# Sixteen more first products of the experts per layer, made during the routing and kept in DRAM until their dense step

## The chip, the cores and the metric

One Trainium2 chip, one core, one launch. The metric is the time of the program on the device in microseconds (us). The engines are TensorE (PE in the rows; PEld is its weight loads), VectorE (DVE), ScalarE (ACT), GpSimd (POOL) and SyncE (SP), which issues most of the DMAs.

## The reference, cut to what matters

Two layers: a token mixer, then PEER, a channel mixer that picks experts by product keys. For each block of 128 tokens and each of 8 heads:

```python
q = (xt @ w_q).reshape(n, PEER_HEADS, 2, PEER_DHALF)
s = jnp.einsum('nhpd,hpkd->nhpk', q, keys)
sv, si = lax.top_k(s, PEER_TOPK)                 # 16 of 128, twice
cand = sv[:, :, 0, :, None] + sv[:, :, 1, None, :]
cs, ci = lax.top_k(cand.reshape(n, PEER_HEADS, -1), PEER_TOPK)
gate = jax.nn.softmax(cs, axis=-1)               # 16 of 16384 experts a head
a = jnp.einsum('nd,nhkd->nhk', xt, u[eidx])      # first product
w = gate * jax.nn.gelu(a, approximate=False)
return jnp.einsum('nhk,nhkd->nd', w, v[eidx])    # second product
```

There are 512 latent and, in layer 0, 256 context tokens.

## The kernel before

**Two ways for the experts.** Three of the four latent blocks (384 tokens, ND) are computed *densely*, for all 16384 experts, in 128 steps of 128 experts. The fourth latent block, and in layer 0 the two context blocks, *gather* the rows of u and v that were chosen: gather(), one "row" at a time, which is an indirect DMA of 512 KB from GpSimd into a ring of five buffers (uv) and one VectorE operation on it (junkv, line 1023, for u; pacc, line 1036, for v). A block has 256 rows; layer 0 has 768 in all, layer 1 256.

**One dense step j.** The *first product* z = gelu(u_j x) has 24 matmuls of 384 columns in three passes (proj2, line 217): weights and tokens are each split into two parts, hi (a cast on ScalarE) and lo (a subtraction on GpSimd or VectorE). Then dense_w multiplies z by the gates (dz, line 1168) and splits the result into dw (1171, 1172). The *second product* adds w v_j into six PSUM banks, dacc, with 18 matmuls of 512 columns (dense_v, line 1178). The first product runs 21 steps (layer 0) or 28 steps (layer 1) ahead of the second, since the first 18 or 27 (UPRE) are made during the routing and wait in SBUF in dz tiles; they get their gelu in dense_w, in place. The last 4 steps' second products are done block by block at the end.

**The stages of peer().** (1) route(): query projections, top-k of the scores, the selection (select(), tiles named sel, dgt, fij) and, for each of the three dense blocks, gate_build(), which makes the dense gate matrix with 32 *units* of two matmuls gds and four gps, and writes it to DRAM (gd). That makes 96 units a layer; below they are counted from 1. Behind it in the program come the UPRE first products (tiles wraw, whi, wlo, dA). beside() lets 78 rows of layer 0 (GROWS) run next to the 96 units. (2) The dense steps; each releases further rows by a quota, behind its dw. (3) A residual add (hm, hr), the next layer's norms, keys and values.

**What sets the order.** All of it is written once in program order; the framework then orders each engine's instructions by a simulated timeline and by priority. So the order on an engine is fixed before the run, and an engine takes its instructions strictly one after the other: what stands behind a waiting instruction waits too. Sixty-four rows (LATE) of layer 0 are left for the next layer's mixer.

Of the kernel before, what the change touches and what calls it, by code (L numbers as in the profile page):

```python
# [9 lines left out]
F32 = mybir.dt.float32  # L10
# [12 lines left out]
ND = 384  # L23
# [5 lines left out]
GROWS = 78, 0  # L29
# [2 lines left out]
NLAT = 5  # L32
FIRST = 1, 1, 0, 1, 0, 1, 0, 1, 0, 1, 0, 1, 1, 0, 0, 0
XA, VPRE = 2, 2
UEXT = 3, 1
TAIL = 4
GEND = 124
# [73 lines left out]
class Kern:  # L111
    def __init__(self, ctx, tc, a, dbg=None):
        self.ctx, self.tc, self.nc, self.a = ctx, tc, tc.nc, a
        self.dbg = dbg or {}
        E = ctx.enter_context
        self.pc = E(tc.tile_pool(name="cst", bufs=1, reuse_waits="tile"))
        self.pg = E(tc.tile_pool(name="gat", bufs=1, reuse_waits="tile"))
        self.px = self.xt = E(tc.tile_pool(name="xt", bufs=1, reuse_waits="tile"))
        self.dr = E(tc.tile_pool(name="dr", bufs=1, space=bass.MemoryType.DRAM))
        self.wk = None  # L120
        nc = self.nc
        self.tables()
        self.cst = self.pc.tile([128, CST_N], F32, name="cst")
        self.ident = self.c("ident")
        self.eps = self.pc.tile([128, 1], F32, name="eps")
        nc.vector.memset(self.eps, EPS)
        self.one = self.c("ones")[:, 0:1]
        self.modd = self.dr.tile([2, 2, 6 * D], F32, name="modd")
        self.hd = self.dr.tile([768, D], F32, name="hd")
        self.x2d = self.dr.tile([768, D], F32, name="x2d")  # L130
        self.h1 = self.dr.tile([768, D], F32, name="h1")
        self.gd = self.dr.tile([ND // 16, 128, 128, 16], F32, name="gd")
        self.yd = self.dr.tile([2, D, 768], F32, name="yd")
        self.bd = self.dr.tile([ND // 128, 1024, 256], BF16, name="bd")

    def consts(self):
# [979 lines left out]
    def halves(self, src, shape, eng):  # L1116
# [6 lines left out]
        eng.tensor_tensor(lo, raw, hi.bitcast(F32), op=OP.subtract)  # L1123
        return hi, lo

    def dense_u(self, j, u, A, xt):


        nc = self.nc
        self.proj2(A, u, xt, ND)  # L1130
        if j % (self.ahead + 1) <= self.upre:
            z = self.dz.tile([128, ND], F32, name="dz", tag="dz", bufs=self.upre + 1)
        else:
            z = self.dn.tile([128, ND], F32, name="dz", tag="dze", bufs=self.ahead - self.upre)
        if j < self.ahead:
            nc.scalar.copy(z, A)
        else:
            nc.scalar.activation(z, A, AF.Gelu)  # L1138
        return z
# [3 lines left out]
        return self.halves(self.a["pr_v"][r:r + 128, :], [D], self.nc.vector)  # L1143

    def ahead_u(self, l, n, pda, xt, z, eng):
        u = self.halves(self.a["uT"][l, n], [8, 128], eng)
        A = pda.tile([128, ND], F32, name="dA", tag="dA", bufs=2)
        z[n] = self.dense_u(n, u, A, xt)
# [10 lines left out]
    def dense_w(self, j, z):  # L1159
        nc = self.nc  # L1160
        JG = self.jg
        if j > 0 and j % JG == 0:
            self.load_gates(j, range(3))
        if j < self.ahead:
            with self.tc.issue_after(self.lastexp.ins):
                nc.scalar.activation(z, z, AF.Gelu)
        z3 = z.rearrange("p (c t) -> p c t", t=16)
        nc.vector.tensor_tensor(z3, z3, self.G[:, :, j % JG, :], op=OP.mult)  # L1168
        wh, wl = (self.dn.tile([128, ND], F32R, name="dw", tag="dw" + x, bufs=2) if j < 128 - TAIL else
                  self.dz.tile([128, ND], F32R, name="dw", tag="dz", bufs=self.upre + 1) for x in "hl")  # L1170
        nc.scalar.copy(wh, z)  # L1171
        i = nc.vector.tensor_tensor(wl, z, wh.bitcast(F32), op=OP.subtract)  # L1172
        return wh, wl, i
# [166 lines left out]
    def peer(self, l, xt, bb, gat, rows, done, late, put):  # L1340

        tc, nc = self.tc, self.nc
        PS = bass.MemoryType.PSUM
        nd = ND // 128
        nb = 4
        upre = self.upre = UPRE[l]
        self.ahead = upre + UEXT[l]
        self.jg = JGS[l]  # L1350
        with tc.tile_pool(name="dz", bufs=1, reuse_waits="tile") as self.dz:
            with self.mixing(), self.phase("rt"):
                pool, tag = ((self.wk, "sel"), (self.pg, "uv"))[l]
                alloc = lambda: pool.tile([128, D], F32, name="sel", tag=tag, bufs=5)
                self.gate_consts()
                step = [0]

                def beside(hot):

                    step[0] += 1  # L1360
                    if step[0] * GROWS[l] // 96 > (step[0] - 1) * GROWS[l] // 96:
                        with tc.issue_after(hot.ins):
                            next(rows)

                sel = self.route(l, xt, nb, nd, alloc, lambda *a: self.gate_build(*a, beside))
                if l == 0:
                    self.mod(1, [0, 1])
                z = {}
                for j in range(upre):
                    u = self.parts(self.weight(self.a["uT"][l, j], [128, 8, 128]), (nc.gpsimd, nc.vector)[j % 2])  # L1370
                    z[j] = self.dense_u(j, u, self.pj([128, ND], "dA"), xt)
            gat += [(bb + b, LAT, sel[b]) for b in range(nd, nb)]
            left, done = 256 * len(gat) - done - GROWS[l] - late, 0
            with tc.tile_pool(name="dn", bufs=1, reuse_waits="tile") as self.dn, \
                    tc.tile_pool(name="pda", bufs=1, space=PS, reuse_waits="tile") as pda, \
                    self.phase("d2"), tc.tile_pool(name="pd", bufs=1, space=PS, reuse_waits="tile") as pd:
                acc = [pd.tile([128, 2, 512], F32, name="dacc%d" % b) for b in range(nd)]
                self.load_gates(0, [0, 1])
                for n in range(upre, self.ahead):
                    self.ahead_u(l, n, pda, xt, z, (nc.gpsimd, nc.vector)[(n - upre) % XA])  # L1380
                vs = {n: self.v_rows(l, n) for n in range(VPRE)}
                self.load_gates(0, [2])
                w = {0: self.dense_w(0, z.pop(0))}
                last = []
                for j in range(128):
                    if j + self.ahead < 128:
                        self.ahead_u(l, j + self.ahead, pda, xt, z, nc.gpsimd)
                    if j == TJ:
                        self.tables(True)
                    if j + 1 < 128:  # L1390
                        w[j + 1] = self.dense_w(j + 1, z.pop(j + 1))
                    wj = w.pop(j)
                    v = vs.pop(j) if j in vs else self.v_rows(l, j)
                    if j < 128 - TAIL:
                        for b in range(nd):
                            self.dense_v(j, b, wj, v, acc)
                    else:
                        last.append((j, wj, v))
                    with tc.issue_after(wj[2].ins):
                        while done < min(left * (j + 2) // GEND, left):  # L1400
                            next(rows)
                            done += 1
                for b in range(nd):
                    for j, wj, v in last:
                        self.dense_v(j, b, wj, v, acc)
                m5 = self.row5(l, LAT)
                for b in range(nd):
                    put(bb + b, self.resid(m5, acc[b].rearrange("p h d -> p (h d)"), bb + b))
# [139 lines left out]
```

## Time and profile before

| | |
|---|---|
| timed runs | 4202.59, 4206.1, 4202.59 us (median 4202.59) |
| profiled execution | 4207.51 us, span 4205.7 us |
| busy | PE 91%, PEld 78%, DVE 79%, POOL 54%, ACT 36% of the span |
| chain that ended last | PE 58%, DVE 16%, DMA 11%, issue 8%, POOL 6% |
| layer 0: gate units, dense steps | 1162 to 1387 us, 1420 to 2405 us |
| layer 1: gate units, dense steps | 3036 to 3237 us, 3245 to 4199 us |

The busy share is a mean over stages with different limits. A matmul's duration overlaps the next one's, so the price of matmuls is read from how many pass in a stretch without a gap.

### The profile page before, as it was taken

Reading aid. Unit: us, or ns where it says so; the run is one execution under the profiler, and the core shown is the slowest. Engines: PE = TensorE matmul, PEld = TensorE weight load, DVE = VectorE, ACT = ScalarE, POOL = GpSimd, SP = SyncE. Lnnn points to the kernel's source line nnn. Section 1 sums busy time; section 2 is a strip of 40 time slices with the busy share of each in tenths; the row PEclk is TensorE's granted clock in tenths of the full one; section 3 lists DMA queues with packets and bytes.
Section 4 is the critical chain, followed back from the end, with each engine's and each line's share of the span. In section 5 each row is a group of like instructions: output and inputs, shape, how many; then the busy total and the mean of one; then the engine's idle time right before and its main releaser. Section 6 shows DMA issues by size and latency. Waiting matters only on the chain.

```text
span 4205.7 us, 56328 instructions
## 1 busy us (share of the span) xinstructions
PE 3816.9 (91%) x19774; PEld 3259.6 (78%) x19780; DVE 3316.6 (79%) x5835; ACT 1508.1 (36%) x2746; POOL 2261.8 (54%) x1644
## 2 busy tenths in 40 slices
PE   8988776769888799999999889999989999999999
PEld 5776554547777699988999767777877899999987
DVE  4359888866998899989999987537875977777788
ACT  3322322312146333333333324332356333333333
POOL 1016777542454587877888563004531666666664
PEclk9999888879999999999999999999999999999999
DMA  5556898783449999999999995423346988787878
GB/s 192 172 200 209 308 322 307 253 287 121 149 161 398 367 332 334 332 324 333 346 339 331 341 333 194 158 85 111 111 160 235 346 279 285 275 290 273 282 268 313
DMA packets 389674, 1099.30 MB, mean 261 GB/s; under 512 B 32959, under 2 KB 140807, under 8 KB 383246
## 3 DMA queue, kind: packets, MB, share of 16 engines
q0 software_dynamic: 147456, 536.94, 35.2%
q1 hardware_dynamic: 232142, 497.95, 34.6%
q10 hardware_dynamic: 9792, 60.82, 3.5%
q8 instruction: 155, 2.54, 0.2%
q14 instruction: 129, 1.06, 0.1%
HBM read 1024.18 MB, written 71.40 MB: 260 GB/s over the span
## 4 chain that ended last, share of the span: by engine, by line
PE 58%; DVE 16%; DMA 11%; issue 8%; POOL 6%; ACT 2%; SPq 0%; ACTq 0%; POOLq 0%; DVEq 0%
PE dacc L1178 20%; PE dA L217 18%; POOL uv L1010 4%; DMA uv<-in_pr_u_dram,ix 3%; PE ops L223 3%; DMA uv<-in_pr_v_dram,ix 3%; PE pqps L217 2%; DVE junkv L1023 2%; PE gps L1108 2%; DMA draw<-in_uT_dram 1%; PE oo L1335 1%; DVE pacc L1036 1%; PE gds L1091 1%; PE modps L252 1%; PE oqps L210 1%
## 5 line engine op out<-in xcount | busy, mean ns | idle before, releaser
L1178 PE MATMUL dacc<-dhi,dw 128*128 128x512 f32 x3072 | 983.7, 390 | 3.4 <-ACT dw L1171 1.9
L1010 POOL DMA_INDIRECT uv<-in_pr_u_dram,ix x512 | 669.4, 1307 | 447.7 <-DVE pa L1023 316.0
L1010 POOL DMA_INDIRECT uv<-in_pr_v_dram,ix x512 | 680.0, 1328 | 408.0 <-DVE pacc L1036 281.9
L1023 DVE CUSTOM_DVE_ANT_0 junkv<-uv,x 128x1024 bf16<-128x1024 f32 x512 | 692.6, 1353 | 65.0 <-DMA uv<-in_pr_u_dram,ix 60.9
L1036 DVE SCALAR_TENSOR_TENSOR pacc<-uv,pw,pacc 128x1024 f32<-128x1024 f32 x508 | 701.5, 1381 | 39.3 <-DMA uv<-in_pr_v_dram,ix 35.4
L1178 PEld LDWEIGHTS dacc<-dhi,dw 128*128 128x128 f32 x3072 | 576.5, 188 | 119.5 <-ACT dw L1171 2.2
L1123 POOL TENSOR_TENSOR dlo<-draw,dhi 128x1024 fp32r<-128x1024 f32 x210 | 545.0, 2596 | 194.9 <-ACT dhi L1122 191.4
L1122 ACT CAST dhi<-draw 128x1024 fp32r<-128x1024 f32 x467 | 489.0, 1050 | 404.9 <-issue 179.5
L1178 PE MATMUL dacc<-dlo,dw 128*128 128x512 f32 x1536 | 601.6, 392 | 5.2 <-DVE dlo L1123 5.2
L1168 DVE TENSOR_TENSOR dz<-dz,dG 128x384 f32<-128x384 f32 x256 | 416.9, 1642 | 73.6 <-ACT dz L1138 71.8
L1171 ACT CAST dw<-dz 128x384 fp32r<-128x384 f32 x256 | 131.5, 514 | 721.2 <-PE dacc L1178 694.3
L1123 DVE TENSOR_TENSOR dlo<-draw,dhi 128x1024 fp32r<-128x1024 f32 x257 | 331.9, 1292 | 17.7 <-ACT dhi L1122 16.1
L217 PE MATMUL dA<-xth,dlo 128*128 128x384 f32 x1688 | 328.1, 335 | 19.0 <-POOL dlo L1123 19.0
L217 PE MATMUL dA<-xth,dhi 128*128 128x384 f32 x1688 | 334.6, 340 | 5.1 <-ACT dhi L1122 5.1
L1178 PEld LDWEIGHTS dacc<-dlo,dw 128*128 128x128 f32 x1536 | 288.2, 188 | 63.8 <-DVE dlo L1123 7.6
L217 PE MATMUL dA<-xtl,dhi 128*128 128x384 f32 x1688 | 326.9, 334 | 0.0
L217 PEld LDWEIGHTS dA<-xth,dhi 128*128 128x128 f32 x1688 | 305.7, 189 | 21.6 <-ACT dhi L1122 5.5
L217 PEld LDWEIGHTS dA<-xth,dlo 128*128 128x128 f32 x1688 | 296.5, 188 | 20.0 <-POOL dlo L1123 20.0
L217 PEld LDWEIGHTS dA<-xtl,dhi 128*128 128x128 f32 x1688 | 296.4, 188 | 0.0
L1172 DVE TENSOR_TENSOR dw<-dz,dw 128x384 fp32r<-128x384 f32 x256 | 154.4, 603 | 150.3 <-ACT dw L1171 150.3
L196 POOL TENSOR_TENSOR wlo<-wraw,whi 128x1024 fp32r<-128x1024 f32 x55 | 132.8, 2416 | 246.7 <-ACT whi L195 129.6
L1108 PEld LDWEIGHTS gps<-ghot 128*128 128x128 f32 x1536 | 205.0, 195 | 70.7 <-issue 39.0
(339 smaller groups left out, 6072.2 us busy)
## 6 DMA issues: line engine op xcount, KB each, us to landing
draw<-in_pr_v_dram SPq DMA_DIRECT2D x256, 512.0 KB
draw<-in_uT_dram SPq DMA_DIRECT2D x211, 512.0 KB
wraw<-in_wb_dram SPq DMA_DIRECT2D x150, 512.0 KB
gd<-gch ACTq DMA_DIRECT2D x48, 1024.0 KB
dG<-gd SPq DMA_DIRECT2D x30, 1536.0 KB
wraw<-in_mod_t_dram SPq DMA_DIRECT2D x48, 512.0 KB
wraw<-in_uT_dram SPq DMA_DIRECT2D x45, 512.0 KB
wraw<-in_mod_w_dram SPq DMA_DIRECT2D x32, 512.0 KB
```

What stands on the lines that cost most here:

```text
L196: eng.tensor_tensor(lo, raw, hi.bitcast(F32), op=OP.subtract)
L217: self.nc.tensor.matmul(ps, w[wi][:, k, :], x[xi][:, k, 0:T], start=(i == 0), stop=(i == 23))
L1010: nc.gpsimd.indirect_dma_start(out=t, out_offset=None, in_=a[table], in_offset=bass.IndirectOffsetOnAxis(ap=ix[:, c:c + 1], axis=0))
L1023: nc.vector.tensor_tensor_reduce(out=junk, in0=u, in1=x, op0=OP.mult, op1=OP.add, scale=1.0, scalar=0.0, accum_out=A[:, c:c + 1])
L1036: nc.vector.scalar_tensor_tensor(acc, v, W[:, c:c + 1], acc, op0=OP.mult, op1=OP.add)
L1108: nc.tensor.matmul(ps[0][:, t0 % 8 + t, :], h[0][:, t, :], h[1][:, t, :], start=True, stop=True)
L1122: nc.scalar.copy(hi, raw)
L1123: eng.tensor_tensor(lo, raw, hi.bitcast(F32), op=OP.subtract)
L1168: nc.vector.tensor_tensor(z3, z3, self.G[:, :, j % JG, :], op=OP.mult)
L1171: nc.scalar.copy(wh, z)
L1172: i = nc.vector.tensor_tensor(wl, z, wh.bitcast(F32), op=OP.subtract)
L1178: self.nc.tensor.matmul(acc[b][:, h, :], w[wi][:, 128 * b:128 * b + 128], v[vi][:, 512 * h:512 * h + 512], start=(j == 0 and i == 0), stop ...
```

## The change

During the routing, behind the UPRE products, 16 further first products are made in each layer. They are those of the steps in self.spill: about evenly spread over the steps that had their first product made among the dense steps (every sixth or seventh). VectorE copies each from PSUM to SBUF (zs) and SyncE writes it to DRAM (zd, 196 KB). In the step in which the first product would have been made, ahead_u loads it into its z tile instead; dense_w gives it its gelu in place. Apart from that, the 78 rows of beside() are spread over the last 80 of the 96 units instead of all 96. The split of the 16 products is on GpSimd in layer 0 and on VectorE in layer 1.

```diff
+USP = 16, 16
+        self.zd = self.dr.tile([2, max(USP), 128, ND], F32, name="zd")
+    def z_tile(self, j):
+        if j % (self.ahead + 1) <= self.upre:
+            return self.dz.tile([128, ND], F32, name="dz", tag="dz", bufs=self.upre + 1)
+        return self.dn.tile([128, ND], F32, name="dz", tag="dze", bufs=self.ahead - self.upre)
     def ahead_u(self, l, n, pda, xt, z, eng):
+        if n in self.spill:
+            z[n] = self.z_tile(n)
+            self.nc.sync.dma_start(z[n], self.zd[l, self.spill.index(n)])
+            return
     def dense_w(self, j, z):
-        if j < self.ahead:
+        if j < self.ahead or j in self.spill:
             with self.tc.issue_after(self.lastexp.ins):
                 nc.scalar.activation(z, z, AF.Gelu)
     def peer(...):
+        self.spill = [self.ahead + (127 - self.ahead) * k // USP[l] for k in range(USP[l])]
                     step[0] += 1
-                    if step[0] * GROWS[l] // 96 > (step[0] - 1) * GROWS[l] // 96:
+                    u = step[0] - 16
+                    if u > 0 and u * GROWS[l] // 80 > (u - 1) * GROWS[l] // 80:
                         with tc.issue_after(hot.ins):
                             next(rows)
+                for k, j in enumerate(self.spill):
+                    u = self.parts(self.weight(self.a["uT"][l, j], [128, 8, 128]), (nc.gpsimd, nc.vector)[l])
+                    A = self.pj([128, ND], "dA")
+                    self.proj2(A, u, xt, ND)
+                    t = self.wk.tile([128, ND], F32, name="zs", tag="pq", bufs=2)
+                    nc.vector.tensor_copy(t, A)
+                    nc.sync.dma_start(self.zd[l, k], t)
```

The order moves in both layers' routing and dense stages; the rest of the program keeps its order. First place: TensorE in layer 0's gate units, around the 23rd of the 96 (gds and gps are a unit, dA a first product). Before:

```order
L1108 MATMUL gps<-ghot 128x128 x4
L1091 LDWEIGHTS gbits
L1091 MATMUL gds<-gB,gbits 128x512
L1091 LDWEIGHTS gbits
L1091 MATMUL gds<-gB,gbits 128x512
L1108 MATMUL gps<-ghot 128x128 x4
```

After:

```order
L1110 MATMUL gps<-ghot 128x128 x4
L219 MATMUL dA<-xth,wlo 128x384 x3
L219 MATMUL dA<-xth,whi 128x384 x8
L219 MATMUL dA<-xtl,whi 128x384 x7
L1093 LDWEIGHTS gbits
L1093 MATMUL gds<-gB,gbits 128x512
L1093 LDWEIGHTS gbits
L1093 MATMUL gds<-gB,gbits 128x512
L1110 MATMUL gps<-ghot 128x128 x4
```

Before, units 13 to 96 of layer 0 had no first-product matmul and units 2 to 12 had 14 to 34 each; now units 2 to 33 have them, 18 in most of the later ones. In layer 1 it is units 2 to 12 before, and 2 to 30 now.

Second place: VectorE at the end of layer 0's dense stage, from its last dw to the residual adds (dlo is the split of v, bfc, snr, snp, snk constants of the next mixer, xn a norm). Before:

```order
L1172 TENSOR_TENSOR dw<-dz,dw 128x384
L1036 SCALAR_TENSOR_TENSOR pacc<-uv,pw,pacc 128x1024
L1123 TENSOR_TENSOR dlo<-draw,dhi 128x1024
L1036 SCALAR_TENSOR_TENSOR pacc<-uv,pw,pacc 128x1024 x2
L1123 TENSOR_TENSOR dlo<-draw,dhi 128x1024
L1036 SCALAR_TENSOR_TENSOR pacc<-uv,pw,pacc 128x1024 x2
L1123 TENSOR_TENSOR dlo<-draw,dhi 128x1024
L1036 SCALAR_TENSOR_TENSOR pacc<-uv,pw,pacc 128x1024 x10
L1213 TENSOR_SCALAR bfc<-cst 128x128 x4
L1052 TENSOR_TENSOR hm<-dacc_10210,m_18853 128x1024
```

After, from the last split of v:

```order
L1125 TENSOR_TENSOR dlo<-draw,dhi 128x1024
L1038 SCALAR_TENSOR_TENSOR pacc<-uv,pw,pacc 128x1024 x9
L1221 TENSOR_SCALAR bfc<-cst 128x128
L1038 SCALAR_TENSOR_TENSOR pacc<-uv,pw,pacc 128x1024
L1221 TENSOR_SCALAR bfc<-cst 128x128 x3
L1038 SCALAR_TENSOR_TENSOR pacc<-uv,pw,pacc 128x1024 x4
L1213 TENSOR_SCALAR snr<-snr 128x16
L381 SCALAR_TENSOR_TENSOR xn<-xn,rstd,mr 128x1024
```

and, after the other constants and the second context norm:

```order
L1218 TENSOR_TENSOR snr<-snr,snp 128x16
L1215 CAST snp<-snr 128x16
L1216 SCALAR_TENSOR_TENSOR snk<-snp,cst,snk 128x16
L1038 SCALAR_TENSOR_TENSOR pacc<-uv,pw,pacc 128x1024 x30
L1054 TENSOR_TENSOR hm<-dacc_10755,m_18918 128x1024
L1054 TENSOR_TENSOR hm<-dacc_10756,m_18918 128x1024
```

Between the last dw and the first hm there are 15 rows before and 48 after; the context norms and the constants have moved ahead of hm. Counted over the whole layer, the rows begun when VectorE reaches the first, the 65th and the last of the 128 dw are 350, 532 and 688 before, and 344, 510 and 655 after.

Third place: ScalarE in layer 1's dense steps, around a step whose first product is loaded (dhi are casts of u and v). After:

```order
L1142 ACTIVATE dz<-dA 128x384
L1179 CAST dw<-dz 128x384
L1124 CAST dhi<-draw 128x1024 x2
L1142 ACTIVATE dz<-dA 128x384
L1174 ACTIVATE dz<-dz 128x384
L1179 CAST dw<-dz 128x384
L1124 CAST dhi<-draw 128x1024
L1179 CAST dw<-dz 128x384
```

The gelu of the loaded tile (L1174) stands some 20 steps before its step, directly ahead of a dw cast; before, each step had one gelu from dA, one dw and two dhi.

## Rows read from the trace of the kernel before

**Rows 1.** Stages: window, length, busy us per engine (instructions), granted clock, DMA share, GB/s.

```profile
1500.00:2380.00 880.00, 877.24 (x4393) 792.63 (x4392) 817.11 (x785) 320.18 (x430) 686.79 (x410) 1.00 0.93 336
...
3260.00:4074.00 814.00, 812.32 (x4106) 738.96 (x4105) 646.05 (x650) 293.93 (x393) 535.70 (x305) 1.00 0.82 287
```

**Rows 2.** The same view over gate units: layer 0's 11, 21, 64; layer 1's.

```profile
1162.50:1239.40 76.90, 62.87 (x362) 58.30 (x362) 73.75 (x222) 33.04 (x56) 40.60 (x44) 0.95 0.41 144
1239.40:1284.60 45.20, 35.59 (x211) 27.57 (x211) 41.75 (x69) 23.86 (x36) 21.53 (x19) 0.85 0.83 302
1284.60:1387.00 102.40, 92.49 (x637) 73.89 (x637) 89.46 (x149) 65.76 (x95) 41.41 (x43) 1.00 1.02 403
3036.20:3112.50 76.30, 66.07 (x379) 61.36 (x379) 70.47 (x207) 37.81 (x68) 41.55 (x41) 0.93 0.29 99
3112.50:3237.00 124.50, 120.89 (x847) 98.42 (x847) 58.12 (x84) 89.35 (x130) 1.79 (x2) 1.00 0.59 224
```

**Rows 3.** The same view, line 217 alone, then line 1178 alone: PE, PEld, clock, DMA.

```profile
3300.00:3700.00 400.00, 209.66 (x1158) 203.47 (x1159) 1.00 0.83 293
...
3300.00:3700.00 400.00, 206.00 (x866) 161.46 (x864) 1.00 0.83 293
4080.00:4140.00 60.00, 60.00 (x266) 49.68 (x265) 1.00 0.94 341
```

**Rows 4.** The same view on VectorE: line 1095 (a unit each), then 1023 (rows).

```profile
3112.50:3237.00 124.50, 58.12 (x84) 1.00 0.59 224
...
1162.50:1239.40 76.90, 10.97 (x18) 0.95 0.41 144
1284.60:1387.00 102.40, 52.67 (x86) 1.00 1.02 403
```

**Rows 5.** Timeline of VectorE, end of layer 0's dense stage: start, length, operation, wait.

```profile
2381.12 0.56 DVE L1172 TENSOR_TENSOR dw<-dz,dw 128x384 fp32r<-128x384 f32 x1 [0.67 <-ACT dw L1171]
...
2391.28 3.96 DVE L1036 SCALAR_TENSOR_TENSOR pacc<-uv,pw,pacc 128x1024 f32<-128x1024 f32 x3
...
2405.30 2.61 DVE L1036 SCALAR_TENSOR_TENSOR pacc<-uv,pw,pacc 128x1024 f32<-128x1024 f32 x2 [1.75 <-DMA uv<-in_pr_v_dram,ix]
...
2408.68 1.23 DVE L1052 TENSOR_TENSOR hm<-dacc,m 128x1024 f32<-128x1024 f32 x1 [0.23 <-DMA m<-modd]
```

**Rows 6.** Groups by line, VectorE, 1500 to 2290, then 2300 to 2376: busy, mean ns.

```profile
L1036 DVE SCALAR_TENSOR_TENSOR pacc<-uv,pw,pacc 128x1024 f32<-128x1024 f32 x137 | 217.7, 1589 | 1.0
...
L1168 DVE TENSOR_TENSOR dz<-dz,dG 128x384 f32<-128x384 f32 x95 | 157.7, 1659 | 38.6 <-ACT dz L1138 38.6
...
L1036 DVE SCALAR_TENSOR_TENSOR pacc<-uv,pw,pacc 128x1024 f32<-128x1024 f32 x32 | 41.0, 1280 | 0.0
```

**Rows 7.** Timeline of TensorE, same place: last second product, context and latent work.

```profile
2404.85 0.39 PE L1178 MATMUL dacc<-dhi,dw 128*128 128x512 f32 x1
...
2429.10 9.43 PE L210 MATMUL okps<-xt,wraw 128*128 128x256 f32 x32 [1.10 <-ACT xt L390]
...
2440.09 1.91 PE L388 MATMUL xps<-cst,xn 128*128 128x128 f32 x16
...
2453.53 5.43 PE L210 MATMUL okps<-xt,wraw 128*128 128x384 f32 x16 [1.10 <-ACT xt L390]
```

**Rows 8.** Timeline of GpSimd, same place: the first and last of five gathers.

```profile
2395.04 1.01 POOL L1010 DMA_INDIRECT uv<-in_pr_v_dram,ix  x1 [0.30 <-issue]
...
2400.85 1.56 POOL L1010 DMA_INDIRECT uv<-in_pr_v_dram,ix  x1 [0.30 <-issue]
```

**Rows 9.** Layer 1, dense: SP and ScalarE timelines; then gathers, median us to landing.

```profile
3602.68 0.33 SPq L1119 DMA_DIRECT2D draw<-in_pr_v_dram  x1
...
3603.67 0.49 ACT L1138 ACTIVATE dz<-dA 128x384 f32<-128x384 f32 x1 [0.29 <-PE dA L217]
3607.57 0.51 ACT L1171 CAST dw<-dz 128x384 fp32r<-128x384 f32 x1 [3.40 <-PE dacc L1178]
...
uv<-in_pr_u_dram,ix POOLq DMA_INDIRECT x122, 5.9
```

More of the change, by code (lines that the diff above doesn't have):

```diff
@@ L1130, in dense_u @@
         self.proj2(A, u, xt, ND)
[L1131 to L1134, printed above, removed]
+        z = self.z_tile(j)
         if j < self.ahead:
```

## The prediction

> **What bounds the kernel now.** I read the busy times by stage first. While an expert layer runs its dense steps, TensorE has no gap: 877.24 of 880 us in layer 0 and 812.32 of 814 us in layer 1 [rows 1]. Building the gate matrices before them is a different place. In layer 1 TensorE is busy 120.89 of 124.5 us there; in layer 0 the same work, with gathered rows beside it, takes 102.40 us for 64 units with TensorE at 92.49 and VectorE at 89.46, and the eleven units before, which share VectorE with the top-k selection, take 76.9 us with TensorE at 62.87 and VectorE at 73.75 [rows 2]. So there are three kinds of place: dense (TensorE), selection (VectorE), plain gate units (TensorE in layer 1, VectorE and TensorE nearly together in layer 0). At the end of layer 0's dense stage a fourth thing decides: VectorE works through gathered rows ahead of the residual add that opens the next layer [rows 5].
>
> **The price of one first product.** In 400 us of layer 1's dense stage there are 866 matmuls of the second product and 1158 of the first; 18 of the former make a step, so 48.1 steps of 8.31 us. After the last first product the second ones run at 266 in 60 us, 4.06 us a step [rows 3]. A first product costs 4.25 us, 0.177 us a matmul, and 16 cost **68 us**.
>
> **Dense, both layers: -68 us each.** TensorE is the bound, and the 16 products leave it. Their load, cast and split leave with them. What comes in their place, a 196 KB load, a gelu on ScalarE of 0.49 us as before, needs no TensorE.
>
> **Layer 1, routing: +67 us.** The order puts the 16 products behind unit 11, into units that had none. Before, 84 such units took 124.5 us, 1.48 us each [rows 2, 4], with TensorE idle 3.6 us in all: 18 of them can hide 0.8 us. VectorE gains a split and a PSUM copy, some 1.2 + 0.7 us, beside a unit of 5.7 us of TensorE in which it has only 0.69 us of its own [rows 4]: covered. Layer 1 is a trade of equal time on the same bound engine.
>
> **Layer 0, routing: +56 us.** (a) Units 1 to 11: their nine rows (18 records of two kinds, 10.97 us [rows 4]) go, since rows now begin with unit 17. But the same number of selection operations stands there as in layer 1, some of them pulled in from the units behind, and layer 1 takes 76.3 us for these eleven units without any row, against 76.9 [rows 2]. I take -1; if TensorE's own work (259 matmuls at 0.177 and 11 units at 1.48, together 62 us) set the pace it would be -15. (b) The next 21 units: 45.2 us before [rows 2]; now they carry 375 matmuls of first products, 66 us, over 21 x 1.48 = 31 us of gates: 97.5 us, so +52. Their rows hide under that. (c) The last 64 units: 43 rows stood in them (86 records of two kinds, 52.67 us [rows 4]), now 47: 4 x 1.3 = +5. Bounds for the sum: +42 (with -15 in a) and +64 (nothing hidden).
>
> **Layer 0, the end of dense: +34 us.** This is what the diff doesn't show. The row quota per step is unchanged, but the order has VectorE later with its rows: in the last dense step it has begun 655 rows, before it was 688. All 704 that belong to the stage still stand ahead of the first residual add. So behind the last dw there are 48 rows instead of 15, 30 of them in one run, and TensorE has long finished. Before, from the last dw (2381.12) to the first hm (2408.68) was 27.6 us, TensorE ending at 2405.2 [rows 5, 7]. A row costs VectorE 1.28 us with GpSimd quiet [rows 6], the gathers are issued 1.45 us apart when they wait for nothing (2395.04 to 2400.85, four gaps) [rows 8], and the last ten rows before hm took 16.6 us, 1.66 each, with waits on landing [rows 5]. 33 rows are 42 to 55 us; I take the gathers' pace, +48. Some of it comes back: before, TensorE did the context tokens' transposes, keys and values between hm and the first latent transposes (2440.09) and reached the latent keys at 2453.53, 44.8 us after hm [rows 7]. Now the context norms stand among the rows, and behind hm stand some 10 us to the first latent transposes (four of VectorE's ten operations at 1.2, the norm's statistics, the norm, GpSimd's add), then the context keys (9.43 from 2429.10 [rows 7]), the values (some 7) and three transposes with a copy (4): about 31 us. That gives back 14 (8 to 20). Net +34, bounds +20 and +47.
>
> **Where the freed time does not go.** With 27 fewer rows inside the dense steps VectorE is no bound there. It is also freed: its multiply of z takes 1.66 us and a row 1.59 while GpSimd splits weights, against 1.28 for a row when GpSimd has no splits [rows 6]. On 16 steps that is some 2 us each. But the 33 rows stand behind the last dw in a fixed order and can't use it, so nothing of it is in the sum.
>
> **A new wait.** ScalarE's gelu of a loaded z stands straight ahead of a dw cast. In layer 1 the load's place on the SP queue is at about 3602.7, ScalarE's free place from 3604.2 to 3607.57 (until then it waited for TensorE), and gathers of 512 KB land 5.9 us after issue [rows 9]. That is 1.8 us late, against some 2.9 us of slack in a step of 4.06. Covered, thinly: I put +3 on both layers together. The Trainium skill (DMA: Bandwidth & Descriptors, Anatomy of one DMA) prices a transfer at about 2 us fixed plus its bytes: 2.5 us here, an estimate by that page, with which ScalarE would not be late, the +3 would be 0 and rival 3 below would fall away; no run here yet shows a load of this size.
>
> **Sum.** Layer 0: +56 - 68 + 34 = +22. Layer 1: +67 - 68 + 3 = +2. Together +24 on the profiled execution's 4207.51 us, which gives 4231.5. That execution was 4.9 us above the median of the timed runs (4202.59), so on their scale **4227 us**, 0.6% slower. Its own bounds: -9 (42 - 68 + 20 and layer 1 at -3) and +63 (64 - 60 + 47 and layer 1 at +12), 4194 to 4266.
>
> **Rivals.** (1) *Idle time is filled, faster.* TensorE is idle 14.0 + 9.6 + 9.9 us in layer 0's gate stage and 10.2 + 3.6 in layer 1's [rows 2], 47 us. If the 32 products fill all of it, routing grows by 136 - 47 = 89, dense falls by 136, the tail adds 34: -13, 4190 us. It decides in the eleven selection units, where half of that idle time is: it needs them to fall to TensorE's own pace. Against it: the products stand behind them in the order, and layer 1's row for these units. (2) *Selection gets faster in layer 0 only, little or no difference.* Without its rows the eleven units fall to 62 us: -14 to my sum, 4213, and 4199 with the tail at its lower bound. For it: VectorE was at 73.75 of 76.9 there, and the nine rows in it were 11 us. Against it, again layer 1's 76.3. (3) *ScalarE waits for z, more slowly.* If landings take 9 us under load instead of 5.9, a product-free step loses about 2 us: 32 x 2 = +64 and, with TensorE later at the last dw and half of the tail hidden so, some 4270. Against it: layer 0 loads its z's 10 us and more ahead. That the change would not move the work is excluded: the order has 32 stores and 32 loads, and the same 6144 first-product matmuls.
>
> **How the numbers follow.** A measurement of this kernel tells about 0.2% (8.4 us) from no change, so no difference is 4194 to 4211. My forecast and its neighbourhood above 4211: 0.55; rival 3: 0.09; rival 2 and the lower part of my own bounds: 0.20; rival 1: 0.16. Slower 0.64, within 0.2% 0.20, faster 0.16. The range that leaves out rival 3's upper part and most of rival 1 is 4197 to 4262.
>
> **What would show it.** Right: the first gate units of the changed layer 0 still near 76 us; units 12 to 32 at 4.6 us with TensorE at work throughout; dense steps without a first product at 4.1 us and the dense stage 68 us shorter up to its last dw; then some 75 us from the last dw to hm, with TensorE idle for about 50 of them and its clock granted at the lower level when it returns; layer 1 equal to within 5 us from first product to end. Wrong: a selection stretch near 62 us (rival 2), ScalarE waiting on zd loads with TensorE waiting behind it (rival 3), or hm less than 50 us behind the last dw.

## The result, and the profile after

The changed kernel took **4255.3 us** (median of four runs, 4250.4 to 4257.5) against 4203.7 us for the kernel before in the same comparison: a ratio of 1.0116, interval 1.0102 to 1.0131. It is 1.2% slower, some 50 us, where the prediction said 24 us. The profiled execution took 4257.5 us, 50.0 us more than the one of before, so the two traces show the whole difference.

The table cuts both traces at the same instructions. "Keys" is the first matmul of the latent keys of layer 1's attention, "scores" the first of layer 1's expert routing.

| stretch (us) | before | changed | difference |
|---|---|---|---|
| layer 0, first gate product to first dense step | 256.5 | 311.7 | +55.2 |
| layer 0, first dense step to last dw | 962.1 | 901.6 | -60.5 |
| last dw to hm | 27.6 | 97.8 | +70.2 |
| hm to keys | 44.9 | 33.2 | -11.7 |
| keys to scores | 409.2 | 409.7 | +0.5 |
| layer 1, scores to first dense step | 384.7 | 447.1 | +62.4 |
| layer 1, first dense step to last dw | 924.4 | 859.8 | -64.6 |
| last dw to the end | 33.8 | 33.8 | 0 |

In front of the first row the changed kernel is 1.4 us ahead. Layer 1 is a trade of equal time (-2.2). All of the loss is in layer 0 and just behind it, and most of it lies between the last dw and the keys: 72.5 us before, 131.0 now.

The gate stages of the changed kernel by windows (columns: window, its length, busy time of PE, PEld, DVE, ACT, POOL with instructions, granted clock, DMA share, GB/s): units 1 to 11, 12 to 32 and 33 to 96 of layer 0. They answer to the first three of [rows 2].

```profile
core 0: us, PE busy (x) PEld busy (x) DVE busy (x) ACT busy (x) POOL busy (x), PEclk, DMA share, GB/s
1161.10:1235.10 74.00, 64.20 (x371) 59.53 (x371) 73.20 (x217) 36.76 (x60) 44.14 (x39) 0.95 0.35 122
1235.10:1329.10 94.00, 93.62 (x587) 87.24 (x586) 43.57 (x67) 38.62 (x47) 48.26 (x29) 1.00 0.73 253
1329.10:1438.40 109.30, 92.41 (x638) 73.88 (x637) 94.10 (x158) 65.50 (x95) 44.01 (x47) 1.00 0.98 379
```

The units with first products are filled by TensorE (93.62 of 94.00 us), and VectorE, busy 43.57, has half of them free. In the last 64 units it is VectorE at 94.10 and the DMA engines at 0.98 that are full, as before. Layer 1's units 12 to 32 and the rest, which answer to the last two of [rows 2]:

```profile
3162.90:3259.30 96.40, 95.55 (x594) 88.06 (x593) 38.70 (x52) 37.70 (x49) 2.42 (x2) 1.00 0.52 185
3259.30:3351.40 92.10, 90.70 (x637) 74.05 (x637) 43.57 (x63) 66.07 (x95) 0.00 (x0) 1.00 0.56 217
```

The two dense stages up to their last dw, same columns, as [rows 1]:

```profile
1472.80:2374.40 901.60, 893.55 (x4411) 799.53 (x4411) 821.00 (x853) 332.15 (x457) 669.43 (x401) 1.00 0.93 335
3362.10:4221.90 859.80, 857.53 (x4217) 766.83 (x4218) 713.62 (x756) 318.39 (x437) 585.05 (x334) 1.00 0.88 310
```

TensorE has no gap in them, as before. Now the place where the time went. VectorE from the last dw of layer 0 to hm, a selection from its timeline (start, length, line, operation, out<-in, count, in brackets the idle time before and what ended it); [rows 5] is the same stretch before.

```profile
2374.36 0.55 DVE L1180 TENSOR_TENSOR dw<-dz,dw 128x384 fp32r<-128x384 f32 x1
...
2402.58 1.28 DVE L1038 SCALAR_TENSOR_TENSOR pacc<-uv,pw,pacc 128x1024 f32<-128x1024 f32 x1 [3.24 <-DMA uv<-in_pr_v_dram,ix]
...
2410.05 1.28 DVE L1038 SCALAR_TENSOR_TENSOR pacc<-uv,pw,pacc 128x1024 f32<-128x1024 f32 x1 [1.19 <-DMA uv<-in_pr_v_dram,ix]
2412.72 1.28 DVE L1038 SCALAR_TENSOR_TENSOR pacc<-uv,pw,pacc 128x1024 f32<-128x1024 f32 x1 [1.39 <-DMA uv<-in_pr_v_dram,ix]
...
2414.00 1.28 DVE L381 SCALAR_TENSOR_TENSOR xn<-xn,rstd,mr 128x1024 f32<-128x1024 f32 x1
...
2420.34 2.97 DVE L1218 TENSOR_TENSOR snr<-snr,snp 128x16 f32<-128x16 f32 x1
...
2466.96 5.25 DVE L1038 SCALAR_TENSOR_TENSOR pacc<-uv,pw,pacc 128x1024 f32<-128x1024 f32 x4 [0.18 <-DMA uv<-in_pr_v_dram,ix]
2472.12 2.35 DVE L1054 TENSOR_TENSOR hm<-dacc,m 128x1024 f32<-128x1024 f32 x2
```

49 rows of 1.28 us (63 us) stand there, waits for their gathers, three weight splits, and some ten us of operations that belong to the next layer (xn, snr and their like). The section on the change counted 48 rows; the trace has 49 ahead of the first hm, against 15 before (a sixteenth stood just behind it), so 34 more there and 33 more behind the last dw. SyncE meanwhile loads for the next layer, from 2393.8 on; TensorE's last second product ends at 2397.9:

```profile
2393.84 1.46 SPq L363 DMA_DIRECT2D mr<-modd  x2
2395.36 2.88 SPq L1475 DMA_DIRECT2D xn<-h  x2
...
2399.04 1.61 SPq L189 DMA_DIRECT2D wraw<-in_wb_dram  x3
```

Each of these is 512 KB, as a gather is, and the rows of 2402 to 2413 come 2.5 us apart. The DMA engines are full there and not behind (the columns are those of the gate stages above; then TensorE's timeline, which waits through it):

```profile
2398.00:2420.00 22.00, 1.19 (x6) 1.19 (x7) 14.17 (x18) 3.29 (x8) 11.12 (x10) 0.55 1.00 398
2420.00:2472.00 52.00, 0.78 (x4) 0.38 (x2) 41.93 (x36) 0.00 (x0) 34.64 (x27) 0.50 0.87 305
```

```profile
2473.49 1.94 PE L390 MATMUL xps<-cst,xn 128*128 128x128 f32 x8 [52.71 <-DVE hm L1054]
```

It waited 52.71 us for hm. Its clock was granted at 0.50, the lower of its two levels, from 2424 to 2472, where it did nothing, and up to 2489 while it worked again. That adds nothing that shows to the loss: over the ten us of the context keys (from 2484) it was 0.75, before (from 2429) 0.76, so both kernels ran about as much of that work at the lower level.

### The profile page after: what moved, and what is told of

Its sections match the earlier page's. It is cut to its first block, busy times and chain, and to the rows that moved or that the text cites. A ratio compares the mean times of both kernels' runs of the same rounds, so it can differ in the third digit from the quotient of the medians.

```text
span 4255.8 us, 56481 instructions
## 1 busy us (share of the span) xinstructions
PE 3809.8 (90%) x19780; PEld 3251.4 (76%) x19780; DVE 3273.4 (77%) x5883; ACT 1506.4 (35%) x2746; POOL 2236.2 (53%) x1628
## 4 chain that ended last, share of the span: by engine, by line
PE 56%; DVE 15%; DMA 13%; issue 9%; POOL 6%; ACT 1%; SPq 0%; POOLq 0%; ACTq 0%; DVEq 0%
PE dacc L1186 18%; PE dA L219 17%; POOL uv L1012 4%; DMA uv<-in_pr_u_dram,ix 4%; DMA uv<-in_pr_v_dram,ix 4%; PE ops L225 3%; PE pqps L219 2%; PE gps L1110 2%; DVE junkv L1025 1%; PE oo L1343 1%; PE gds L1093 1%; DMA draw<-in_uT_dram 1%; DVE pacc L1038 1%; PE ops L1313 1%; PE modps L254 1%
## 5 line engine op out<-in xcount | busy, mean ns | idle before, releaser
L1025 DVE CUSTOM_DVE_ANT_0 junkv<-uv,x 128x1024 bf16<-128x1024 f32 x512 | 702.0, 1371 | 70.2 <-DMA uv<-in_pr_u_dram,ix 66.1
L1125 POOL TENSOR_TENSOR dlo<-draw,dhi 128x1024 fp32r<-128x1024 f32 x178 | 467.0, 2624 | 306.4 <-ACT dhi L1124 245.0
L1124 ACT CAST dhi<-draw 128x1024 fp32r<-128x1024 f32 x435 | 453.9, 1049 | 334.5 <-issue 127.6
L1176 DVE TENSOR_TENSOR dz<-dz,dG 128x384 f32<-128x384 f32 x256 | 279.1, 1107 | 64.9 <-ACT dz L1142 35.5
L198 POOL TENSOR_TENSOR wlo<-wraw,whi 128x1024 fp32r<-128x1024 f32 x71 | 171.6, 2418 | 275.9 <-ACT whi L197 138.1
L219 PE MATMUL dA<-xth,dlo 128*128 128x384 f32 x1432 | 279.2, 336 | 18.7 <-POOL dlo L1125 18.6
L219 PE MATMUL dA<-xth,dhi 128*128 128x384 f32 x1432 | 284.5, 340 | 7.2 <-ACT dhi L1124 7.2
L219 PE MATMUL dA<-xtl,dhi 128*128 128x384 f32 x1432 | 279.4, 336 | 0.0
L219 PEld LDWEIGHTS dA<-xth,dhi 128*128 128x128 f32 x1432 | 259.5, 189 | 22.5 <-ACT dhi L1124 9.1
L219 PEld LDWEIGHTS dA<-xth,dlo 128*128 128x128 f32 x1432 | 252.5, 189 | 20.2 <-POOL dlo L1125 19.8
L219 PEld LDWEIGHTS dA<-xtl,dhi 128*128 128x128 f32 x1432 | 253.3, 189 | 0.1
```

The costliest lines, as they stand in the source:

```text
L219: self.nc.tensor.matmul(ps, w[wi][:, k, :], x[xi][:, k, 0:T], start=(i == 0), stop=(i == 23))
L1025: nc.vector.tensor_tensor_reduce(out=junk, in0=u, in1=x, op0=OP.mult, op1=OP.add, scale=1.0, scalar=0.0, accum_out=A[:, c:c + 1])
L1124: nc.scalar.copy(hi, raw)
```

## The experiments

The theory after the result, T: moving a first product is an even trade for TensorE. What is lost is the cover of layer 0's rows: the dense stage is some 60 us shorter, fewer rows fit beside it, and each of the 33 rows that slide behind the last dw is paid in full. R1 to R6, C, P, D, V and G are the theories that the expectations below name. The same cuts for every run (us, from the profiled executions; ratios with their intervals come from the timed runs, each against the kernel before on the same chip):

| run | gate stage 0 | dense 0 | dw to hm | hm to keys | keys to scores | ratio to before |
|---|---|---|---|---|---|---|
| before | 256.5 | 962.1 | 27.6 | 44.9 | 409.2 | 1 |
| changed | 311.7 | 901.6 | 97.8 | 33.2 | 409.7 | 1.0116 (1.0102 to 1.0131) |
| 1, layer 1 only | 258.5 | 966.0 | 28.1 | 44.6 | 409.1 | 0.9994 (0.9982 to 1.0005) |
| 2, layer 0 only | 310.1 | 897.7 | 97.7 | 32.7 | 405.1 | 1.0099 (1.0082 to 1.0116) |
| 3, rows later only | 240.7 | 967.3 | 53.8 | 34.2 | 406.2 | 1.0014 (1.0001 to 1.0027) |
| 4, 33 rows past hm | 312.9 | 897.3 | 32.2 | 42.6 | 450.5 | 1.0067 (1.0050 to 1.0084) |
| 5, rows beside products | 318.9 | 901.3 | 67.9 | 33.8 | 410.4 | 1.0062 (1.0044 to 1.0081) |
| 6, 33 rows left out | 313.1 | 894.5 | 33.2 | 42.0 | 410.4 | 0.9979 (0.9964 to 0.9994) |
| 7, next loads held back | 311.3 | 896.7 | 86.4 | 54.2 | 407.5 | 1.0135 (1.0112 to 1.0159) |
| 8, half rows | 312.7 | 898.5 | 88.6 | 32.8 | 410.0 | 1.0096 (1.0074 to 1.0118) |
| 9, 7 and half vector work | 310.9 | 897.5 | 73.7 | 53.5 | 411.1 | one run |
| 10, 7 and half gathers | 309.7 | 901.1 | 68.9 | 49.7 | 404.0 | one run |
| 11, 5 and 17 rows past hm | 315.4 | 900.0 | 27.9 | 42.3 | 420.6 | 1.0036 (1.0023 to 1.0049) |

**1. Layer 1 alone.**

```diff
-USP = 16, 16
+USP = 0, 16
-                    u = step[0] - 16
-                    if u > 0 and u * GROWS[l] // 80 > (u - 1) * GROWS[l] // 80:
+                    if step[0] * GROWS[l] // 96 > (step[0] - 1) * GROWS[l] // 96:
```

> The 16 stored first products are made in layer 1 alone, and layer 0 is as in the kernel before (its rows again spread over 96 gate units). Theory T (the loss is layer 0's 33 rows behind the last dense step; the move of a first product is itself an even trade): within 5 us of the kernel before, layer 1's gate stage about 64 us longer and its dense stage about 64 us shorter. Rival R1 (each moved product costs some 1.5 us by its copy, store, load and wait): about 25 us slower than before.

Measured: no difference (ratio 0.9994). Layer 1's stage from scores to the first dense step took 449.1 us, +64.4, its dense stage 860.4, -64.0. A moved product costs nothing by itself. R1 is out.

**2. Layer 0 alone.** `USP = 16, 0`, nothing else.

> The 16 stored first products are made in layer 0 alone. Theory T: all of the loss is here, 47 to 55 us slower than the kernel before, with about 48 rows behind the last dw and 95 to 100 us from there to the first residual add. Rival R1 (cost per moved product): half of the loss, about 25 us.

Measured: 0.99% slower, 44.5 us by the medians, a little under T's 47 to 55, with the changed kernel's way from dw to hm (97.7 us). The loss is layer 0's. R1 is out here too.

**3. The rows' new place alone.** `USP = 0, 0`, the rows still over the last 80 units.

> No first product is moved; only the change to the rows' place in layer 0's gate units (over the last 80 units, not over 96) is kept. The order has 681 rows begun at the last dw, 23 behind it (15 in the kernel before, 48 in the changed one). Theory T (each row behind the last dw costs about 1.5 to 2 us, less a part that returns): 8 to 16 us slower than before. Rival R2 (the rows' new place in the gate stage is the cause of the loss): 40 to 50 us slower.

Measured: 0.14% slower, some 6 us; the profiled execution itself was the shortest of its ten. T's sign and size of the stretch held: the eight rows more ahead of hm made the way from dw to keys 88.0 us instead of 72.5. What T did not say is that the gate stage gains 15.8 us by the rows' leaving its first units, so that the sum fell under T's 8 to 16. R2 is out as the main cause. The products of layer 0 with the rows left over all 96 units were not run; by the counts, six of the 33 rows were already late at the first dense step (344 begun instead of 350), and the other 27 were lost in the dense stage.

**4. 33 rows moved past the add.** `LATE = 97` instead of 64.

> The changed kernel with 97 instead of 64 rows left for the attention stage of layer 1, so that 16 and not 48 rows stand between the last dw and the first residual add; nothing else differs. Theory T: from the last dw to that add falls from 97.7 us to 30 to 40, and the attention stage, in which rows end some 250 us before the expert routing begins, hides most of the 33: 40 to 60 us faster than the changed kernel, near the kernel before. Rival R3 (the 33 rows cost the same wherever they stand, since the attention of the last blocks waits for them): the add comes earlier, but the first routing scores of layer 1 come within 10 us of where they do in the changed kernel.

Measured: only half a per cent faster than the changed kernel. From dw to hm it is 32.2 us, as T said, but from keys to scores 450.5 instead of 409.7. The longest wait of TensorE in the attention stage (who waited, for whom, us in total, times, longest):

```profile
PE xps L390 <- POOL xn L383: 39.6, 1, 39.6
```

It waits once, 39.6 us, for the norm of the last latent block, which needs these rows. T's forecast of 40 to 60 us failed. R3 is nearer, though from the last dw to the scores it was 15.4 us shorter than in the changed kernel, more than R3's 10: that stage had room for the 64 rows that it had, and for few more.

**5. More rows beside the products.**

```diff
-GROWS = 78, 0
+GROWS = 111, 0
-                    u = step[0] - 16
-                    if u > 0 and u * GROWS[l] // 80 > (u - 1) * GROWS[l] // 80:
+                    s = min(max(step[0] - 11, 0), 21), max(step[0] - 32, 0)
+                    q = min(max(step[0] - 12, 0), 21), max(step[0] - 33, 0)
+                    for _ in range(47 * s[0] // 21 + s[1] - 47 * q[0] // 21 - q[1] if GROWS[l] else 0):
```

> The changed kernel with the rows of layer 0's gate stage released otherwise: 47 beside the 21 units that carry the moved first products and 64 beside the 64 units behind them (78 over the last 80 units in the changed kernel). In the order 362 rows are begun at the first dense step (344 before) and 31 stand behind the last dw (48 before). Theory T (the rows lost the dense steps that covered them; the product units, where VectorE was busy 43.57 of 94 us, could cover some): the gate stage no longer by over 6 us, from last dw to hm some 34 us less (17 rows at 2.0 us), of which a fifth comes back behind it: 20 to 34 us faster than the changed kernel. Rival R4 (beside the products rows cost as much, since GpSimd's splits and the gathers collide there): the gate stage longer by 17 to 34 us and no gain.

Measured: some 20 us faster than the changed kernel (1.0062 against 1.0116); 18 fewer rows behind the last dw took 29.9 us off the way to hm. Units 12 to 32 there:

```profile
1235.00:1338.20 103.20, 96.22 (x587) 88.37 (x586) 89.65 (x112) 38.44 (x48) 89.21 (x52) 0.98 0.90 317
```

They grew from 94.0 to 103.2 us with 21 rows more on VectorE; the gate stage as a whole grew by 7.2 us with 18 rows more, a little over T's 6. VectorE is at 89.65 where it was at 43.57, and GpSimd's records cover 89.21: nearly full. A row costs about 0.4 us here (9.2 / 21 and 7.2 / 18) against 1.8 behind the last dw. T holds. R4's collision is there (a gather takes GpSimd 1.46 us on the mean in these units, 0.95 in the changed kernel's), but not at R4's price of 17 to 34 us, so R4 is out.

**6. 33 rows left out.**

```diff
             for c in range(128):
+                if l == 0 and s == LAT and 16 <= c < 49:
+                    yield
+                    continue
                 v = fetch("pr_v", ix, c)
```

> The changed kernel without 33 of the 48 rows that stand behind the last dw (they are left out of the third block's sum), so 15 remain as in the kernel before. Theory T: the 33 rows are the whole loss: from last dw to hm 30 to 40 us instead of 97.7, and 45 to 60 us faster than the changed kernel, at or just under the time of the kernel before. Rival R5 (something else holds the next layer there, and the rows only lie beside it): less than 25 us faster.

Measured: 60.2 us shorter than the changed kernel in the traces, 0.2% under the kernel before. The last dw and hm:

```profile
2367.05 0.55 DVE L1183 TENSOR_TENSOR dw<-dz,dw 128x384 fp32r<-128x384 f32 x1
...
2400.22 2.35 DVE L1057 TENSOR_TENSOR hm<-dacc,m 128x1024 f32<-128x1024 f32 x2
```

With 33 rows fewer nothing is left of the loss. Nothing else holds the next layer there. R5 is out.

**7. The next layer's loads held back.**

```diff
-        nc.sync.dma_start(h, self.hd[128 * hb:128 * hb + 128, :])
+        self.hr = nc.sync.dma_start(h, self.hd[128 * hb:128 * hb + 128, :])
...
+                with tc.issue_after(self.hr.ins):
+                    xt = self.odd(xs, hl, lambda: [next(rows, None) for _ in range(LATE)])
```

(and the same around the context's row and token loads ahead of it)

> The changed kernel with all loads of layer 1's attention (ten of 512 KB among them) queued on SP behind the residual add's own loads; between the last dw and the first hm then stand only the 48 rows and three weight splits, and the context norms and the mask and sink operations stand behind hm. Theory C (the tail was 22 us over my forecast because the next stage's loads and VectorE operations share it, about half by each): 75 to 83 us from last dw to hm instead of 97.7, and hm to the latent keys back at 40 to 50 us instead of 33, so that the program's time moves by less than 12 us. Rival P (a row simply costs 2.0 us there, whatever stands beside it): 90 us or more from last dw to hm, and the program 5 to 15 us slower.

Measured: 86.4 us from dw to hm, between C's 83 and P's 90.

```profile
2367.08 0.55 DVE L1180 TENSOR_TENSOR dw<-dz,dw 128x384 fp32r<-128x384 f32 x1
...
2453.52 2.35 DVE L1054 TENSOR_TENSOR hm<-dacc,m 128x1024 f32<-128x1024 f32 x2
```

The next stage's work among the rows cost 11.4 us, not 22, and about that much came back in the changed kernel (hm to keys 33.2 instead of 44.9). The rows alone are dearer than the 1.45 us of the prediction: (86.4 - 27.6) / 34 = 1.73. From hm to the keys it took 54.2 us, not 40 to 50: the context norms' loads went out only from 2459.6, and TensorE's first transposes came 24.8 us behind hm, before 13.0. The program was 0.2% slower than the changed kernel by the medians, which the intervals do not separate. Its stretch with nothing but rows, by windows, and GpSimd's group there (line, engine, operation, count, busy us, mean ns, idle before and its releasers):

```profile
2392.00:2440.00 48.00, 0.00 (x0) 0.00 (x0) 36.91 (x29) 0.00 (x0) 38.20 (x29) 0.53 0.90 311
...
L1012 POOL DMA_INDIRECT uv<-in_pr_v_dram,ix x29 | 39.3, 1355 | 9.8 <-issue 7.3 <-DVE pacc L1038 1.6 <-DMA uv<-in_pr_v_dram,ix 0.9
```

29 rows in 48 us, 1.66 each: a gather's 1.36 us on GpSimd and the 0.3 us to the next. GpSimd is all but always at it; VectorE waits for landings.

**8. Rows of half width on VectorE.**

```diff
+                n = 512 if l == 0 and s == LAT and 16 <= c < 64 else D
-                    nc.vector.scalar_tensor_tensor(acc, v, W[:, c:c + 1], acc, op0=OP.mult, op1=OP.add)
+                    nc.vector.scalar_tensor_tensor(acc[:, 0:n], v[:, 0:n], W[:, c:c + 1], acc[:, 0:n],
+                                                   op0=OP.mult, op1=OP.add)
```

> The changed kernel, in which the 48 rows behind the last dw are added over half their width (VectorE 0.65 us instead of 1.28 for one; the other half of their sum is left out); the gathers still bring whole rows. Theory D (the gathers' landing sets the pace of the rows there): from last dw to hm less than 12 us shorter. Rival V (VectorE's own time sets it): 25 to 30 us shorter (48 x 0.63).

Measured: 9.2 us less from dw to hm. VectorE's own time is not what sets the pace; V is out, and D stands so far.

**9 and 10. What sets the gathers' pace.** Both start from experiment 7. In 9 the edit of 8 is added; in 10:

```diff
-            nc.gpsimd.indirect_dma_start(out=t, out_offset=None, in_=a[table],
+            nc.gpsimd.indirect_dma_start(out=t[:, 0:n], out_offset=None, in_=a[table] if n == D else a[table].rearrange("r (h d) -> (r h) d", h=2),
...
```

(n is 512 in the 48 rows; VectorE reads each half row for both halves of its operation)

> The kernel with the next layer's loads held back (86.4 us from last dw to hm, GpSimd issuing one gather after the other, 0.94 to 2.0 us each and 0.3 between them), with the 48 rows added over half their width on VectorE (the other half of their sum left out); the gathers bring whole rows. Theory G (GpSimd's issuing sets the pace there, and VectorE's full-width rows lengthen it): the gathers fall to 0.94 us throughout and hm comes 70 to 78 us behind the last dw. Rival D (the transfer of 512 KB sets the pace): 82 us or more, with the gathers' durations unchanged or GpSimd waiting for buffers.

> The kernel with the next layer's loads held back, with the same 48 gathers bringing half rows (256 KB; other rows of the table than meant, so that the sum is another), each used for both halves, so that VectorE does its full-width operation of 1.28 us. Theory G (GpSimd's issuing, lengthened by VectorE's rows, sets the pace): gathers still alternate up to 1.9 us, and hm stays within 5 us of 86.4 behind the last dw. Rival D (the bytes set it): VectorE's own pace is left, 23 + 38 x 1.3 = about 73 us.

Measured: 73.7 us in 9, as G said; 68.9 in 10, near D's 73. The same 48 us of both, first of 9, then of 10:

```profile
2392.00:2440.00 48.00, 0.00 (x0) 0.00 (x0) 25.99 (x35) 0.00 (x0) 26.45 (x30) 0.51 0.97 366
...
L1012 POOL DMA_INDIRECT uv<-in_pr_v_dram,ix x29 | 27.2, 936 | 13.3 <-DVE pacc L1039 13.3
```

```profile
2392.00:2440.00 48.00, 1.67 (x8) 1.05 (x6) 45.81 (x36) 0.00 (x0) 33.45 (x34) 0.57 0.73 207
...
L1012 POOL DMA_INDIRECT uv<-in_pr_v_dram,ix x33 | 34.1, 1032 | 10.1 <-issue 10.1
L1039 DVE SCALAR_TENSOR_TENSOR pacc<-uv,pw,pacc 128x1024 f32<-128x1024 f32 x35 | 45.0, 1285 | 2.3 <-DMA uv<-in_pr_v_dram,ix 1.2
```

A gather costs GpSimd 1.36 us beside full rows, 0.94 with half the vector work, 1.03 with half the bytes. In 9 GpSimd waits for buffers (13.3 us) and the DMA engines, 0.97 busy at 366 GB/s, look like the next bound; in 10 VectorE does (45.81 of 48). So neither G nor D alone: three resources are close together, and the dearer gather appears only when both are at full size. Why less data makes the issue cheaper stays open. The Trainium skill (SBUF — State Buffer, SBUF: two separate sides) says that VectorE and GpSimd share a pair of ports under an exclusive lock, so that VectorE operations of certain kinds (an fp32 copy within SBUF is the one that it names) can hold up the descriptors of a DMA that GpSimd issues, while transfers and engines do not slow each other. Experiment 9 looks like the first half (1355 to 936 ns), with another operation than the one named there. Whether the lock also makes experiment 10 is not shown: with VectorE's operations as long as before, fewer bytes took 1355 to 1032 ns, and no run tells the issue from the transfer there.

**11. Both relocations.** Experiment 5 with `LATE = 81`.

> The kernel with rows beside the products (31 behind the last dw), with 17 more rows left for the attention stage, so 14 behind the last dw. Theory T with the prices found so far (a row costs about 1.8 us behind the last dw and about 1.25 in the attention stage): 6 to 14 us faster than without the 17, some 4222 to 4230, still slower than the kernel before. Rival R6 (the attention stage hides 17 rows, where 33 were too many): 25 to 30 us faster, about the kernel before.

Measured: 1.0036, by the ratios some 11 us faster than experiment 5, within T's 6 to 14; the profiled execution, the shortest of nine, was 28.8 us shorter than that of 5, as R6 had it. The two traces put some 21 us of that between the last dw and the scores, more than T's price and less than R6's, so T and R6 are not cleanly told apart here. From dw to hm 27.9 us, as before; from keys to scores 10.2 more than in 5, with TensorE's wait:

```profile
PE xps L390 <- POOL xn L383: 12.6, 1, 12.6
```

So the attention stage takes some rows more for little: 17 cost a wait of 12.6 us, 33 one of 39.6. No version with products moved in layer 0 and all rows kept reached the kernel before.

## Why the prediction was right or wrong

**Direction and mechanism were right, one term was mis-sized.** The rows behind the last dw decide, as forecast, and the changed kernel is slower; the time lies in the range. But the change was +50 us, not +24, and the term that was off lies outside its own bounds (+20 to +47): the range held because the bounds of the other terms had widened it.

- *Routing, layer 0, +56:* right, +55.2. Units 1 to 11: -2.7 (forecast -1); 12 to 32: +48.6 (+52), at 4.5 us each; the last 64: +6.9 (+5); from there to the first dense step +2.4, which was not in the sum.
- *Dense, -68 a layer with +3 for the new wait:* -64.6 in layer 1, where TensorE's busy time fell by 65.0, so that a first product was worth 4.06 and not 4.25 us. In layer 0 -60.5 here, while the nine further kernels with the same products moved took 894.5 to 901.3 us, -61 to -68.
- *Routing, layer 1, +67:* +62.4 from scores to the first dense step. Layer 1 as a whole: forecast +2, measured -2.2, and no difference in experiment 1.
- **The failed step: the end of dense in layer 0, +34; it measured +58.5** (70.2 less 11.7). It failed twice over. First, the pace: I took 1.45 us a row from four gathers [rows 8]; the rows at nothing but their own pace cost 58.8 us (experiment 7; 34 rows and not the 33 of the count, 1.73 each), with gathers of 1.36 us and 0.3 between. That is 10.8 us. The ten rows ahead of hm with 1.66 each [rows 5] were the nearer row, and I passed them over. Second, the give-back: I subtracted 14 us for the context norms that now stand among the rows, but put nothing on the stretch that they lengthen. 11.7 did come back behind hm, but the next stage's work, these norms among it, had cost 11.4 ahead of it (experiment 7): together, nothing in the sum. 34 + 10.8 + 14 = 58.8.
- *What ties the runs together:* where the next stage's loads keep their place, each row more ahead of hm cost much the same from dw to keys: 8 rows +15.5 us (experiment 3), 16 rows +29.2 (experiment 5), 34 rows +58.5, that is 1.94, 1.82 and 1.72 us; with 33 of them left out it is 75.2 us, 2.7 over the 72.5 of before.
- *The new wait:* ScalarE does wait for loaded z, more than I thought (us in total, times, longest; layer 1's dense stage, then layer 0's):

```profile
ACT dz L1174 <- DMA dz<-zd: 41.1, 11, 6.4
...
ACT dz L1174 <- DMA dz<-zd: 18.1, 7, 6.6
```

Yet TensorE has 2.3 and 8.0 us without work in these two stages in all (2.0 and 5.8 before). So it is covered, and rival 3, whose 4270 us was the nearest number, has the wrong cause. One of these loads and its use (SyncE, then ScalarE):

```profile
3583.30 0.70 SPq L1152 DMA_DIRECT2D dz<-zd  x1
...
3592.83 0.53 ACT L1174 ACTIVATE dz<-dz 128x384 f32<-128x384 f32 x1 [3.55 <-DMA dz<-zd]
```

It came 9.4 us after its issue. The loads that ScalarE waited for came 3.5 to 9.4 us after issue in layer 1's dense stage (median 4.0) and 5.2 to 11.0 in layer 0's, on both sides of the 5.9 that I took from the gathers [rows 9]. Some reached rival 3's 9 us, and layer 0's were not safe by being issued early, as I had argued; TensorE still did not wait behind them. By the Trainium skill's formula (DMA: Bandwidth & Descriptors, Anatomy of one DMA) it would be 2.5, an estimate for this size; all that ScalarE waited for took longer. That page of the Trainium skill fits the formula to DMAs that GpSimd issues, and these were SyncE's.
- *Rivals 1 and 2* did not come: TensorE's 14.0 us without work in units 1 to 11 of layer 0 became 9.8, and these units took 74.0 us, not 62.
- *The signs to look for* came but for one: 74.0 us for the first units, 4.5 us a unit behind, dense stages 60.5 and 64.6 us shorter, TensorE idle for 52.7 us before hm at the lower clock. The one that did not come was the "some 75" us from dw to hm: it was 97.8.

What stays open: why a gather costs GpSimd less when it brings half the bytes; and where single executions of experiments 3 and 11, 18 and 15 us apart in their ten and nine runs, differ, since one of each was traced. The split of a row's price among GpSimd, VectorE and the DMA engines rests on one run each of experiments 9 and 10.

## What to carry to other kernels

A stage that is full on one engine may be the cover of another engine's work: before work is taken out of it, count what the cover hid, and price each uncovered piece at the pace that it has with everything around it, not at its best. Where work moves from one side of a mark to the other, book it on both sides or on neither. New cover can arise where the work went: here the gate units that received the products took rows at some 0.4 us each, but only when the rows were put there by hand.

## What was not expected of the hardware

- A gather of 128 rows of 4 KB cost GpSimd 0.94 us beside VectorE operations of half width, 1.03 us when it brought 2 KB rows, and 1.36 us on the mean with both at full size (experiments 9, 10 and 7).
- The DMA engines, 0.97 busy, moved 366 GB/s where nothing but gathers ran (experiment 9), and 379 GB/s at 0.98 in the gate units of the changed kernel; where 512 KB loads of the next stage ran beside the gathers (DMA engines 1.00 busy, 398 GB/s), the gathers came 2.5 us apart, 1.66 without them (experiment 7).
